# Who adds the weight sums of the seven-part products: VectorE at fixed places in place of GpSimd, in a one-layer hybrid encoder kernel

## The chip, the cores and the metric

The kernel runs on one core of a Trainium2 chip. The metric is the device time of one execution in microseconds (us); lower is better. The profile names the core's engines: PE is TensorE (matmuls), PEld its weight loads, DVE is VectorE, ACT is ScalarE, POOL is GpSimd, SP is SyncE, whose queue only issues transfers.

## The reference, cut to what matters

One layer over 256 tokens of width 4096, in float32. A combined projection feeds forgetting attention, an RWKV-7 scan and a gate; their gated outputs go through one output projection and a LayerNorm.

```python
proj = jnp.einsum('bsd,dc->bsc', x, w_in)
...
h = jnp.concatenate([fox_out, rwkv_out], axis=-1) * jax.nn.silu(z.astype(f32))
out = jnp.einsum('bsc,cd->bsd', h.astype(x.dtype), w_out)
x = _layernorm(ALPHA * x.astype(f32) + out.astype(f32), ln_gain, ln_bias, LN_EPS).astype(x.dtype)
```

`w_in` has 4096 rows and about 14,500 columns, `w_out` is 4096 by 4096. Reading and multiplying by these two is most of the work.

## The kernel before

**Two stages.** The input projection runs first, over eight groups of heads (`n` from 0 to 7), each in four blocks of 512 columns (`b` from 0 to 3; the text calls them first to fourth block). A block accumulates over 32 row tiles, taken in 16 pairs (`q`). Then comes the output projection.

**A weight pair** is one 512 KB load on SP's queue. Float32 accuracy is had from a high and a low part: ScalarE casts the pair to the high part (`split`, L155), VectorE subtracts it to get the low part (L156), and TensorE does three matmuls for each row tile and token half (`mm`, L161 to L163), twelve a pair. `weights()` keeps three split pairs ready ahead of TensorE; there are four buffers for high and three for low parts.

**Side work in slots.** After every sixth matmul of a pair, thus twice a pair and 32 times a block, `slot()` lets each side generator in `sides` take one step: first `ahead()` (preparing heads), then `gates()` (the forget gate, in group 0), `chain()` (the RWKV work, `rwkv(n)`), `weight_sums()`, and after these the generators that unload blocks and do attention. What a step issues stands in the program behind the splits made so far, and each engine works through its own instructions in that order. So a generator's place in time is set by how many slots it waits (`wait(n)`).

In the third block of a group, `chain()` multiplies the keys' tiles (`gp`, L586), masks the result on VectorE (`gb` and `lt`, L603 and L611), writes it to memory as `nd` and reads it back spread over the partitions as `Nb` (L606, L607; 1 MB a group). The triangular solve (L653, L656) runs on VectorE in the fourth block and the start of the next group; its result goes through memory again (`td` from `xc`, then `T`, L663 and L665), and `T` feeds the matmuls `qt` (L691). GpSimd scales `BK` (L588), mixes `vs` with its shifted copy (L590 to L592) and makes copies between partitions: `hr` (L512), `BKt` (L623), `pT` (L815).

At a block's end ScalarE copies the two accumulators out (`bk`, L1114). There are three such banks, so the second half of the next block's first pair waits for the first of these copies.

**Seven-part products.** In the output projection, two pairs of column blocks (those that start at 3 and 5) do the products of row-tile pairs 4 to 11 as 2 by 2 block products with seven instead of eight multiplications. These need sums of weights. There are 16 sets of them (two starts, eight row-tile pairs), and `weight_sums()` makes them while the input projection runs: for each set it loads four 128x512 tiles of `w_o` into the one buffer `ts` (four transfers of 256 KB, issued from ScalarE's queue by `send`, L846), subtracts four times in place (L856), and writes the four results to memory as two stores of 512 KB (`td`, again from ScalarE's queue). The output projection reads them back in place of plain weights.

Before, GpSimd does the subtractions, and the generator goes on at its own pace: two slots for each load and six more, six after each subtraction and six more, five after each store. That is 54 slots a set, so the sets drift through the groups: one begins 1 2/3 blocks after the other.

Of the kernel before, what the change touches and what calls it, by code (L numbers as in the profile page):

```python
# [14 lines left out]
ALU = mybir.AluOpType  # L15
# [6 lines left out]
G = 16  # L22
# [29 lines left out]
TAIL = 3  # L52
STARTS = (3, 5)
RING = (4, 3)
W = {"fo": 7, "vs": 2, "np": 4, "gp": 5, "tp": 4, "d1": 8, "d2": 12, "xp": 3, "fs": 4, "fp": 5}
NB = D // OB

# [37 lines left out]
def layer(ctx: ExitStack, tc: tile.TileContext, xt, xtok, w_main, w_lora, w_first, muv, w_o, up, par, mulora, fbias, lng, lnb, cst, out):  # L95
    nc = tc.nc
# [8 lines left out]
    def pst(name):  # L105
        return ps.tile([P, 512], F32, tag="ps", name=name)
# [52 lines left out]
    def mm(acc, at, k, hi, lo, o, n):  # L159
        tt = slice(at * P, (at + 1) * P)  # L160
        nc.tensor.matmul(acc[:, :n], xs[k][:, 0, tt], hi[:, o : o + n], start=(k == 0), stop=False)  # L161
        nc.tensor.matmul(acc[:, :n], xs[k][:, 1, tt], hi[:, o : o + n], start=False, stop=False)  # L162
        nc.tensor.matmul(acc[:, :n], xs[k][:, 0, tt], lo[:, o : o + n], start=False, stop=(k == KT - 1))  # L163

    def steps(n, last):
        both = [(j, m) for j in range(n) for m in range(2)]
        return sorted(both, key=lambda t: t[1]) if last else both
# [35 lines left out]
    nc.vector.memset(gneps, GN_EPS)  # L203

    sides = []

    def wait(n):
        for _ in range(n):
            yield
# [4 lines left out]
    def slot():  # L214
        with tc.issue_after(latest[0].ins), tc.issue_after(latest[1].ins):
            for g in list(sides):
                try:
                    next(g)
                except StopIteration:
                    sides.remove(g)  # L220
# [14 lines left out]
    tds = {(b, q): dram.tile([P, 4, OB], F32, name=f"td{b}_{q}") for b in STARTS for q in FEW}  # L235
# [22 lines left out]
    def load():  # L258
        name, src = stream.pop()
        wide = rpool is not None  # L260
        turn_of[0] = (turn_of[0] + 1) % (sum(RING) if wide else RING[0])
        own = turn_of[0] >= RING[0]
        raw = (rpool if own else wpool).tile([P, 1024], F32, tag="we" if own else "wr", name=name, bufs=RING[own])
        nc.sync.dma_start(out=raw[:, : src.shape[1] * OB], in_=src.rearrange("p k c -> p (k c)"))
        raws[name] = raw

    def fetch():
        while len(raws) < (3 if rpool is None else sum(RING) - 1) and stream:
            load()
        job = jobs.pop()  # L270
        name = job[0] if len(job) == 1 else named(*job)
        raw = raws.pop(name)
        if name not in kept:
            ready.append((job, *split(raw, OB if job[0] == "e2" else 2 * OB, name)))
            return
        hl = []
        for j in range(4):
            hl.append(xpool.tile([P, OB], F32R, tag=f"x{4 * kept[name] + j}", name=f"{name}_{j}"))
        for j in range(2):
            r = raw[:, j * OB : (j + 1) * OB]  # L280
            nc.scalar.copy(hl[j], r)
            nc.vector.tensor_tensor(hl[2 + j], r, hl[j].bitcast(F32), ALU.subtract)
        ready.append((job, hl[:2], hl[2:]))

    def weights(job):
        while len(ready) < 3 and jobs:
            fetch()
        got, hi, lo = ready.pop(0)
        assert got == job
        return hi, lo  # L290

    def block(n, b):
        if n == 0 and b == 0:
            return acc_0
        acc = [pp.tile([P, 512], F32, tag="pp", name=f"acc{n}_{b}_{m}") for m in range(2)]
        for q in range(KT // 2):
            hi, lo = weights((f"w{n}_{b}_{q}",))
            for t, (j, m) in enumerate(steps(2, q in (0, KT // 2 - 1))):
                mm(acc[m], m, 2 * q + j, hi, lo, j * OB, OB)
                if t % 2:  # L300
                    slot()
                    if n == G // 2 - 1 and b == 3:
                        paced(2 * q + t // 2)
        return acc
# [141 lines left out]
    def ch(t):  # L446
        return t.rearrange("p (c t) -> p c t", t=C)
# [70 lines left out]
    def left(t, j):  # L518
        return t.rearrange("p u c (x j t) -> p u c j x t", x=2, j=2)[:, :, :, j]

    def prepare(i):
# [30 lines left out]
        for j in range(2):  # L552
            h = HALF[j]
            nc.vector.tensor_tensor(BK[h, :, KB[j][1]], ch(k)[h], ch(eI)[h], ALU.mult)
        yield from wait(W["np"] if n else 2 * W["np"])
        nc.vector.tensor_tensor(hr[:, 0, :], hr[:, 0, :], hr[:, 1, :], ALU.add)
# [15 lines left out]
    def rwkv(n):  # L572
# [5 lines left out]
        lt = [left(LT, j) for j in range(2)]  # L578
        yield from wait(W["gp"])
        gp = [[pst(f"gp{n}_{u}_{j}") for j in range(2)] for u in range(2)]  # L580
# [34 lines left out]
        UV = [UVt[:, :, :, j, :] for j in range(2)]  # L615
        yield from wait(W["tp"])
        BKt = rp.tile([P, 2, NCH - 1, P], F32, tag="shl", name=f"BKt{n}")
# [3 lines left out]
        for a in range(4):  # L621
            for b in range(4):
                nc.gpsimd.tensor_copy(BKt[B * b : B * (b + 1), :, :, B * a : B * (a + 1)], BK[B * a : B * (a + 1), :, : NCH - 1, B * b : B * (b + 1)])  # L623
            if a % 2:
                yield
        yield from wait(W["d1"])

# [43 lines left out]
        for j in range(2):  # L671
# [8 lines left out]
            nc.gpsimd.memset(SV[j][HALF[j], :, 0, :], 0.0)  # L680
        yield from wait(W["d2"] - 1)
        for a in range(4):
# [25 lines left out]

        yield from wait(W["xp"])
        xp = pst(f"xp{n}")  # L710
# [129 lines left out]
        yield from forget()  # L840

    def weight_sums():
        g = nc.gpsimd.tensor_tensor

        def send(out, src):
            tc.keep_in_program_order(nc.scalar.dma_start(out=out, in_=src))  # L846

        for b, q in tds:
            t = rp.tile([P, 4, OB], F32, tag="ts", name=f"ts{b}_{q}")
            for n in range(4):  # L850
                send(t[:, n], w_o[b + n // 2][:, 2 * q + n % 2, :])
                yield from wait(2)
            yield from wait(6)
            b11, b21, b12, b22 = (t[:, n] for n in range(4))
            for o, x, y in ((b11, b12, b11), (b12, b22, b12), (b22, b22, b11), (b21, b21, b22)):
                g(o, x, y, ALU.subtract)  # L856
                yield from wait(6)
            yield from wait(6)
            for n in (2, 0):
                send(tds[b, q][:, n : n + 2], t[:, n : n + 2])  # L860
                yield from wait(5)
# [77 lines left out]
    def paced(k):  # L939
        while len(sent_h) < min(FAR, k * PACE[0] // PACE[1]):  # L940
            sent_h.append(len(sent_h))
            get_h(sent_h[-1])
# [155 lines left out]
    side(gates())  # L1098
    side(chain())
    side(weight_sums())  # L1100
    vt = None
    for n in range(G // 2):
        for b in range(4):
            acc = block(n, b)
            while unloading or b == 2 and n not in turned:
                slot()
            bk = rp.tile([P, 2, OB], F32, tag="bk", name=f"bk{n}_{b}") if n or b else bk_0
            for m in range(2):
                if b == 1:
                    nc.scalar.copy(bk[:, m, : 2 * P], acc[m][:, : 2 * P])  # L1110
                elif not n and not b:
                    nc.scalar.copy(bk[:, m, P:], acc[m][:, :LB])
                else:
                    nc.scalar.copy(bk[:, m, :], acc[m])  # L1114
            if b == 0:
                muvs[n] = rp.tile([P, 2 * P], F32, tag="prod", name=f"muv{n}")
                nc.sync.dma_start(out=muvs[n], in_=muv[n : n + 1, :].to_broadcast([P, 2 * P]))
            if b == 1:
                vd = vds[n % 2]
                bks[n] = bk[:, :, : 2 * P]  # L1120
                nc.sync.dma_start(out=vd[1:].rearrange("(m p) c -> p m c", m=2), in_=bk[:, :, : 2 * P])
                vs_[n] = rp.tile([P, 2, 2 * P], F32, tag="vs", name=f"vs{n}")
                nc.sync.dma_start(out=vs_[n], in_=vd[:S].rearrange("(m p) c -> p m c", m=2))
                while n and 2 * n - 1 not in foxed:
                    slot()
                vt = rp.tile([P, 2, 2 * P], F32, tag="vt", name=f"vt{n}")
                for m in range(2):
                    nc.scalar.copy(vt[:, m, :], acc[m][:, 2 * P :])
            if b != 1:
                unloading.append(n)  # L1130
                side(unload(n, b, bk, vt))
# [55 lines left out]
    for kind, b, q in plan:  # L1187
# [3 lines left out]
        if pair:  # L1191
            n = count[pair] = count[pair] + 1
# [149 lines left out]
    o = slice((NB - 1) * OB, NB * OB)  # L1342
# [96 lines left out]
```

## Time and profile before

| | |
|---|---|
| median of 3 runs | 1931.33 us (1927.58 to 1933.35) |
| the profiled execution | 1930.38 us |
| its span, first to last instruction | 1928.6 us |
| mean granted clock of TensorE | 0.997 |
| subtractions of the sets on POOL (L856) | 64, of 1279 ns at least and 1353 in the median |
| loads of the sets | 64, from 67.0 to 1294.2 us |
| stores of the sets | 32, from 128.9 to 1353.7 us |

A line of the page that groups instructions reads: line, engine, operation, output from inputs by the program's names, shapes, count, then busy time and mean duration in ns, then the idle time of the engine ahead of them and what ended most of it. A line of the waits reads: engine and line, what it waited for, total us, how many times, the longest. A line of the timeline: start and duration in us, engine, line, operation, and in brackets the idle time before it and what ended it; ACTq and SPq are the parts of ScalarE and SP that issue transfers. A line of the windows: the stretch, its length, busy time of PE, PEld, DVE, ACT and POOL with the number of instructions, granted clock, the DMA engines' busy share, and GB/s. DMA lines of the page end with the median time from issue to landing.

### The profile page before, as it was taken

To read this page: it belongs to the slowest core of one execution; us is meant where nothing else is said; L and a number is where in the kernel's file an instruction comes from. 1 tells how busy PE (TensorE), PEld (TensorE's weight loads), DVE (VectorE), ACT (ScalarE), POOL (GpSimd) and SP (SyncE) were. 2 spreads that over 40 slices of the span, in tenths; PEclk is the share of its full clock that TensorE was granted. 3 is DMA by queue.
4 is the path that set the end of the run, shared out by engine and by line. 5 is a ranking of instruction groups with operands and counts; after the bars stand their busy time and mean duration, and the time that the engine had idled before them with its cause. 6 is when DMAs were issued, how large, how long until landed. Compare 5 with 4: busy or idle time off the path is not lost.

```text
span 1928.6 us, 28470 instructions
## 1 busy us (share of the span) xinstructions
PE 1905.0 (99%) x9745; PEld 1574.9 (82%) x9745; DVE 1489.4 (77%) x2469; ACT 1012.8 (53%) x1581; POOL 356.9 (19%) x530
## 2 busy tenths in 40 slices
PE   9999999999999999999999999999999999999998
PEld 9887788888778888887878888888888878878885
DVE  7678778786878687867786878788768775887886
ACT  6554465456535564565355545654565454455552
POOL 0223123120331223213220331232002200000000
PEclk9999999999999999999999999999999999999999
DMA  9678777877787788867887787788767875778883
GB/s 344 190 238 252 227 203 256 249 243 217 233 249 236 220 267 250 253 193 248 246 250 219 246 268 235 221 272 241 235 188 221 288 268 179 265 256 300 293 301 120
DMA packets 288262, 466.76 MB, mean 242 GB/s; under 512 B 144434, under 2 KB 171716, under 8 KB 288116
## 3 DMA queue, kind: packets, MB, share of 16 engines
q1 hardware_dynamic: 274004, 431.03, 72.3%
q10 hardware_dynamic: 14112, 33.90, 4.9%
q8 instruction: 76, 1.25, 0.2%
q14 instruction: 70, 0.57, 0.1%
HBM read 418.43 MB, written 46.42 MB: 241 GB/s over the span
## 4 chain that ended last, share of the span: by engine, by line
PE 90%; DVE 5%; DMA 2%; ACT 1%; issue 1%; SPq 0%; DVEq 0%; POOL 0%; ACTq 0%; POOLq 0%
PE acc L161 22%; PE acc L163 22%; PE acc L162 22%; PE oacc L980 4%; PE oacc L983 4%; PE oacc L981 4%; DMA w<-in_w_main_dram 1%; PE rh L700 1%; PE p L980 1%; PE p L983 1%; PE p L981 1%; PE gp L586 1%; PE up L731 1%; PE sp L741 1%; DVE prod L653 1%
## 5 line engine op out<-in xcount | busy, mean ns | idle before, releaser
L856 POOL TENSOR_TENSOR ts<-ts 128x512 f32<-128x512 f32 x64 | 103.0, 1609 | 251.4 <-DMA ts<-in_w_o_dram 248.4
L815 POOL COPY pT<-lg 32x96 f32<-32x96 f32 x128 | 58.7, 458 | 426.1 <-DVE lg L811 421.4
L653 DVE TENSOR_TENSOR prod<-Nb,xc 128x8 f32<-128x8 f32 (+30 forms) x248 | 83.4, 336 | 3.0
L623 POOL COPY BKt<-BK 32x192 f32<-32x192 f32 x128 | 70.4, 550 | 53.5 <-DVE BK L620 48.5
L656 DVE TENSOR_REDUCE xc<-prod 128x8 f32<-128x16 f32 (+30 forms) x248 | 72.6, 293 | 6.5
L156 DVE TENSOR_TENSOR w_0l<-w,w_0h 128x1024 fp32r<-128x1024 f32 x31 | 39.2, 1266 | 40.8 <-ACT w_0h L155 34.1
L155 ACT CAST w_0h<-w 128x1024 fp32r<-128x1024 f32 x31 | 32.5, 1048 | 64.5 <-DMA w<-in_w_main_dram 57.7
L155 ACT CAST w_6h<-w 128x1024 fp32r<-128x1024 f32 x31 | 32.7, 1055 | 47.1 <-PE acc L162 26.9
L155 ACT CAST w_8h<-w 128x1024 fp32r<-128x1024 f32 x31 | 32.6, 1052 | 45.7 <-DMA w<-in_w_main_dram 16.8
L156 DVE TENSOR_TENSOR w_9l<-w,w_9h 128x1024 fp32r<-128x1024 f32 x31 | 39.1, 1260 | 19.6 <-ACT w_9h L155 8.7
L156 DVE TENSOR_TENSOR w_6l<-w,w_6h 128x1024 fp32r<-128x1024 f32 x31 | 43.0, 1387 | 13.3 <-ACT hry L774 7.3
L1290 POOL CAST zah<-mv 128x1 fp32r<-128x1 f32 x1 | 0.2, 188 | 284.5 <-DVE mv L1285 284.5
L156 DVE TENSOR_TENSOR w_15l<-w,w_15h 128x1024 fp32r<-128x1024 f32 x31 | 39.6, 1277 | 16.5 <-issue 12.6
L156 DVE TENSOR_TENSOR w_11l<-w,w_11h 128x1024 fp32r<-128x1024 f32 x31 | 38.4, 1239 | 17.7 <-PE acc L163 12.0
L156 DVE TENSOR_TENSOR w_10l<-w,w_10h 128x1024 fp32r<-128x1024 f32 x31 | 38.4, 1238 | 17.1 <-ACT w_10h L155 8.1
L155 ACT CAST w_10h<-w 128x1024 fp32r<-128x1024 f32 x31 | 32.6, 1052 | 35.1 <-DMA w<-in_w_main_dram 27.1
L161 PE MATMUL acc<-w_0h,x 128*128 128x512 f32 x124 | 49.9, 403 | 1.1 <-ACT bk L1114 1.0
L163 PE MATMUL acc<-w_5l,x 128*128 128x512 f32 x124 | 48.7, 392 | 1.6 <-DVE w_5l L156 1.6
L155 ACT CAST w_1h<-w 128x1024 fp32r<-128x1024 f32 x31 | 32.7, 1054 | 33.4 <-DMA w<-in_w_main_dram 15.7
L161 PE MATMUL acc<-w_15h,x 128*128 128x512 f32 x124 | 50.1, 404 | 0.0
L155 ACT CAST w_9h<-w 128x1024 fp32r<-128x1024 f32 x31 | 32.6, 1050 | 33.3 <-DMA w<-in_w_main_dram 17.6
L161 PE MATMUL acc<-w_9h,x 128*128 128x512 f32 x124 | 50.0, 403 | 0.0
(1052 smaller groups left out, 6834.6 us busy)
## 6 DMA issues: line engine op xcount, KB each, us to landing
w<-in_w_main_dram SPq DMA_DIRECT2D x496, 512.0 KB, 4.5
wo<-in_w_o_dram SPq DMA_DIRECT2D x96, 512.0 KB, 4.9
ts<-in_w_o_dram ACTq DMA_DIRECT2D x64, 256.0 KB, 3.7
td<-ts ACTq DMA_DIRECT2D x32, 512.0 KB, 4.4
e<-td SPq DMA_DIRECT2D x32, 512.0 KB, 5.2
bt<-bk SPq DMA_DIRECT2D x88, 128.0 KB, 4.5
Nb<-nd SPq DMA_DIRECT2D x16, 512.0 KB
e<-in_w_o_dram SPq DMA_DIRECT2D x16, 512.0 KB, 4.0
```

Of the source, the lines that this page charges most:

```text
L155: latest[1] = nc.scalar.copy(hi[:, :n], src[:, :n])
L156: latest[0] = nc.vector.tensor_tensor(lo[:, :n], src[:, :n], hi[:, :n].bitcast(F32), ALU.subtract)
L161: nc.tensor.matmul(acc[:, :n], xs[k][:, 0, tt], hi[:, o : o + n], start=(k == 0), stop=False)
L162: nc.tensor.matmul(acc[:, :n], xs[k][:, 1, tt], hi[:, o : o + n], start=False, stop=False)
L163: nc.tensor.matmul(acc[:, :n], xs[k][:, 0, tt], lo[:, o : o + n], start=False, stop=(k == KT - 1))
L623: nc.gpsimd.tensor_copy(BKt[B * b : B * (b + 1), :, :, B * a : B * (a + 1)], BK[B * a : B * (a + 1), :, : NCH - 1, B * b : B * (b + 1)])
L653: first = nc.vector.tensor_tensor(prod[:, :, :, s + 1 :], nb[:, :, s : s + 1, s + 1 :].to_broadcast([P, 2, NJ, w]), xc[:, :, :, s + 1 :], ...
L656: solved = nc.vector.tensor_reduce(xc[:, :, :, s : s + 1], prod[:, :, :, s:], AX.X, ALU.add)
L856: g(o, x, y, ALU.subtract)
L980: nc.tensor.matmul(acc, h, hi, start=n[0] == n[1], stop=False)
L981: nc.tensor.matmul(acc, l, hi, start=False, stop=False)
L983: nc.tensor.matmul(acc, h, lo, start=False, stop=not n[0])
```

## The change

The four subtractions of each set move from GpSimd to VectorE. They no longer come a fixed number of slots after the loads. The generator now holds after its loads until the input projection has reached pair 7 (`CALM`) of a given block: in groups 1 to 7 the first and the third block, in group 0 (whose first block has no slots) the second and the third. `where[0]` is the block and pair that `block()` is working on. From there the subtractions follow two slots apart (slots 14, 16, 18 and 20 of the block), the two stores go out at slots 26 and 31, and the next set's loads at slots 36, 38, 40 and 42, which are slots 4 to 10 of the next block. The loads' and stores' engine, sizes and number stay.

```diff
+CALM = 7
...
     sides = []
+    where = [(0, 0, 0)]
...
             hi, lo = weights((f"w{n}_{b}_{q}",))
+            where[0] = n, b, q
...
     def weight_sums():
-        g = nc.gpsimd.tensor_tensor
-
         def send(out, src):
             tc.keep_in_program_order(nc.scalar.dma_start(out=out, in_=src))
 
-        for b, q in tds:
+        places = [(n, b, CALM) for n in range(G // 2) for b in (0 if n else 1, 2)]
+        for (b, q), place in zip(tds, places, strict=True):
             t = rp.tile([P, 4, OB], F32, tag="ts", name=f"ts{b}_{q}")
             for n in range(4):
                 send(t[:, n], w_o[b + n // 2][:, 2 * q + n % 2, :])
                 yield from wait(2)
-            yield from wait(6)
+            while place > where[0]:
+                yield
             b11, b21, b12, b22 = (t[:, n] for n in range(4))
             for o, x, y in ((b11, b12, b11), (b12, b22, b12), (b22, b22, b11), (b21, b21, b22)):
-                g(o, x, y, ALU.subtract)
-                yield from wait(6)
-            yield from wait(6)
+                nc.vector.tensor_tensor(o, x, y, ALU.subtract)
+                yield from wait(2)
+            yield from wait(4)
             for n in (2, 0):
                 send(tds[b, q][:, n : n + 2], t[:, n : n + 2])
                 yield from wait(5)
```

## The prediction

> **What bounds the kernel now.** I began with the page: busy times, the chain, and the group of the line that the change touches.
>
> ```profile
> PE 1905.0 (99%) x9745; PEld 1574.9 (82%) x9745; DVE 1489.4 (77%) x2469; ACT 1012.8 (53%) x1581; POOL 356.9 (19%) x530
> PE 90%; DVE 5%; DMA 2%; ACT 1%; issue 1%; SPq 0%; DVEq 0%; POOL 0%; ACTq 0%; POOLq 0%
> L856 POOL TENSOR_TENSOR ts<-ts 128x512 f32<-128x512 f32 x64 | 103.0, 1609 | 251.4 <-DMA ts<-in_w_o_dram 248.4
> ```
>
> TensorE is busy almost throughout, and the chain runs through it for nine tenths. POOL has 81% of the span free, so taking 103 us from it is worth nothing by itself. The change can only pay where the sums, or their transfers, hold TensorE up. So I read what TensorE waited for.
>
> ```profile
> PE lp L482 <- DVE upl L474: 2.9, 2, 2.3
> PE qt L691 <- DMA T<-td: 2.0, 2, 1.0
> PE acc L163 <- DVE w_7l L156: 1.6, 1, 1.6
> PE acc L161 <- ACT bk L1114: 1.0, 1, 1.0
> PE acc L163 <- DVE w_12l L156: 0.8, 1, 0.8
> ```
>
> These are few and short, but they aren't the whole loss. Groups 1 to 7 do identical work, so I cut the span at the start of each block and compared like with like (columns: stretch, length, busy time per engine, granted clock, DMA share, GB/s).
>
> ```profile
> 207.82:261.98 54.16, 52.15 (x297) 43.02 (x296) 35.88 (x61) 24.50 (x40) 6.78 (x6) 0.97 0.75 226
> 404.09:455.13 51.04, 50.77 (x297) 41.52 (x296) 37.92 (x66) 25.26 (x43) 4.00 (x5) 1.00 0.69 199
> 984.17:1035.34 51.17, 50.83 (x297) 41.44 (x296) 37.96 (x69) 25.70 (x45) 1.40 (x3) 1.00 0.73 214
> 1175.07:1225.25 50.18, 50.18 (x298) 41.68 (x296) 34.56 (x62) 25.40 (x43) 5.44 (x5) 1.00 0.79 244
> 310.29:359.03 48.74, 47.09 (x231) 38.53 (x230) 40.68 (x49) 21.37 (x30) 22.39 (x29) 1.00 0.76 239
> 503.27:553.76 50.49, 48.20 (x231) 39.76 (x230) 37.55 (x52) 18.70 (x25) 17.36 (x27) 0.97 0.65 208
> 888.86:938.54 49.68, 47.05 (x231) 38.39 (x230) 39.64 (x50) 22.23 (x35) 22.82 (x29) 1.00 0.72 224
> 1463.23:1509.69 46.46, 46.46 (x231) 38.53 (x230) 35.90 (x46) 21.39 (x31) 17.49 (x24) 1.00 0.70 209
> 553.76:600.59 46.83, 45.47 (x201) 37.09 (x200) 43.14 (x89) 26.24 (x44) 11.55 (x12) 1.00 0.88 267
> 938.54:984.17 45.63, 45.18 (x202) 37.18 (x200) 37.42 (x81) 21.85 (x36) 10.26 (x12) 1.00 0.89 269
> 1320.02:1364.91 44.89, 44.89 (x202) 37.26 (x201) 37.77 (x87) 23.48 (x37) 4.34 (x10) 1.00 0.85 246
> ```
>
> The first four are first blocks (groups 1, 2, 5, 6), the next four third blocks (1, 2, 4, 7), the last three fourth blocks (2, 4, 6). Each kind has an undisturbed length: 50.18, 46.46 and 44.89 us. The excess over it is what can be won. First blocks: 3.98 + 0.86 + 0.99 = 5.8. Third: 2.28 + 4.03 + 3.22 = 9.5. Fourth: 1.94 + 0.74 = 2.7. Together 18.0 us; the other blocks of these kinds, and the second blocks, are within some tenths of undisturbed.
>
> **Are the sums behind this excess?** The disturbed third blocks are the ones in which POOL's sums run while VectorE is full. Group 4's, around 902 us, beside a split of group 7 with POOL quiet:
>
> ```profile
> 902.55 2.21 DVE L156 TENSOR_TENSOR w_5l<-w,w_5h 128x1024 fp32r<-128x1024 f32 x1
> 902.19 1.48 POOL L856 TENSOR_TENSOR ts<-ts 128x512 f32<-128x512 f32 x1
> 909.44 0.89 POOL L512 COPY hr<-hr 32x16 f32<-32x16 f32 x4
> 910.36 0.17 DVE L556 TENSOR_TENSOR hr<-hr 128x16 f32<-128x16 f32 x1 [3.38 <-POOL hr L512]
> 1483.82 1.22 DVE L156 TENSOR_TENSOR w_9l<-w,w_9h 128x1024 fp32r<-128x1024 f32 x1
> ```
>
> Beside POOL's adds a split takes 2.21 instead of 1.22 us. Further, the short copies of hr wait in POOL's queue behind the sums and the products of vs (L590 to L592), and VectorE waits 3.38 us for them, with w_7l's split queued behind that: that is TensorE's 1.6 us wait. The products of vs stay on POOL; but the undisturbed third blocks hold them too, without this loss, so it takes both. Group 2's 4.03 us has TensorE's 2.3 us wait for upl at its start; after that pause the granted clock of its block is 0.97. I book the 9.5 us as removable.
>
> In group 1's first block it is the sums' stores:
>
> ```profile
> 213.30 0.33 ACTq L846 DMA_DIRECT2D td<-ts  x1
> 215.94 4.67 DMA td<-xc
> td<-xc SPq DMA_DIRECT2D x16, 64.0 KB, 1.5
> ```
>
> The solve's small write lands after 4.67 instead of 1.5 us, right behind a 512 KB store of the sums, and TensorE waits for T. In the new order nothing of the sums lies in a first block's pairs 0 to 6, so I book these 4.0 us as removed too. Groups 2 and 5 lose 0.9 and 1.0 us in first blocks in which VectorE is 3.4 us busier than in the undisturbed one (37.9 against 34.56): again adds on POOL beside a full VectorE, and again gone. What the fourth blocks lose (2.7 us) is the stores' doing, below; I count it as removed here and as a cost there.
>
> **The change, part by part.**
>
> *Off POOL:* 64 adds of 1609 ns. Nothing is gained but what VectorE loses beside them, booked above.
>
> *Onto VectorE:* 64 adds of two SBUF tensors. The nearest row is this one, with the same shape:
>
> ```profile
> L1084 DVE TENSOR_TENSOR res<-res,lg 128x512 f32<-128x512 f32 x15 | 9.9, 685 | 0.0
> ```
>
> 64 x 0.685 = 44 us. What hides it is the idle time of VectorE at the places. The four adds of a set go into weight pairs 7, 8, 9 and 10, one each. Those pairs in an undisturbed first block, a third block, the three pairs behind these, and group 0's third block:
>
> ```profile
> 1384.79:1395.20 10.41, 10.41 (x81) 8.61 (x80) 6.47 (x10) 4.88 (x10) 0.00 (x0) 1.00 0.83 212
> 1483.00:1493.37 10.37, 10.37 (x69) 8.54 (x68) 6.67 (x9) 3.20 (x4) 1.40 (x1) 1.00 0.76 235
> 1493.37:1501.53 8.16, 8.16 (x37) 6.76 (x36) 7.52 (x10) 3.14 (x3) 1.56 (x3) 1.00 0.61 142
> 144.73:154.04 9.31, 8.46 (x37) 6.68 (x36) 9.18 (x15) 3.15 (x3) 0.00 (x0) 1.00 0.73 182
> ```
>
> In a first block VectorE has 10.41 - 6.47 = 3.9 us free in pairs 7 to 9: all adds fit, cost 0. In a third block pairs 7 to 9 have 3.7 us free, the next three 0.64. The third add can land behind the masks of gp (the same slot, the solve's side step first) and the fourth in pair 10, so up to 1.4 us are pushed into pairs 10 to 12. They are covered by the weights split ahead: three pairs are kept ready, so a split may come some 2 to 3 us late before TensorE runs out. Cost 0 in groups 1 to 7; were that cover gone, 0.7 to 1.4 us a block.
>
> Group 0 has no such room: from pair 10 of its third block VectorE is busy 9.18 of 9.31 us (the forget gate's steps share it), and TensorE already waits 0.8 us for w_12l. The two late adds cost between 0 and 1.4; I take +1.0. Group 0's other set sits in its second block, where POOL's adds of the first set now run in the same pairs: what VectorE gets back there is of the size of what it takes on. I take 0; at worst none of it is hidden, 4 x 0.685 = 2.7.
>
> What stands behind an add that waits are VectorE's splits, and behind them TensorE. But no add should wait:
>
> ```profile
> ts<-in_w_o_dram ACTq DMA_DIRECT2D x64, 256.0 KB, 3.7
> ```
>
> A load lands in 3.7 us, and each set's loads go out a block or more before its adds. Only group 0 is closer: its first loads go out in pairs 0 to 3, its second set's in pairs 2 to 5, of the block of their adds. A pair without side matmuls takes 8.16 / 3 = 2.7 us (third row of the fence above), so the last load, two pairs ahead, has 5.4 us.
>
> *The loads and stores, moved along.* ScalarE's queue still issues them, but at other times: stores at slots 26 and 31 of the block with the adds (pairs 13 and 15), the next loads in pairs 2 to 5 of the block after. In first blocks this is quiet. In third blocks the first store falls, every time, into the stretch in which Nb is fetched and the next block's w_0 stands behind it. Before shows this once, in group 2 (ScalarE and the SP queue; then the same stretch of group 7, without a store):
>
> ```profile
> 540.59 1.53 SPq L607 DMA_DIRECT2D Nb<-nd  x2
> 542.91 0.35 ACTq L846 DMA_DIRECT2D td<-ts  x1
> 552.34 1.05 ACT L155 CAST w_0h<-w 128x1024 fp32r<-128x1024 f32 x1 [8.43 <-DMA w<-in_w_main_dram]
> 553.62 0.33 ACTq L846 DMA_DIRECT2D td<-ts  x1
> 550.00:554.00 4.00, 4.00 (x20) 3.29 (x18) 0.58 (x1) 1.51 (x2) 1.73 (x5) 1.00 0.91 370
> 1495.90 1.61 SPq L607 DMA_DIRECT2D Nb<-nd  x2
> 1505.30 1.05 ACT L155 CAST w_0h<-w 128x1024 fp32r<-128x1024 f32 x1 [5.46 <-DMA w<-in_w_main_dram]
> ```
>
> w_0 is there 9.40 us after Nb's issue in group 7, 11.75 in group 2: the store made it 2.35 us later. Counted from the next block's start (553.76 and 1509.69), w_0 came 1.42 us ahead instead of 4.39, so 2.97 us later (Nb itself was late), and the block lost 1.94 us, because ScalarE's bk copies stand behind w_0 and TensorE's second half waits for their bank. So about 1.0 us of lateness is free. With 2.35 us from the store alone, a block loses 1.3. If the store costs only its own transfer time, 0.524 MB at 370 GB/s = 1.4 us, it loses 0.4. I take the middle, 0.85, since both describe the same event: 7 groups x 0.85 = +6.0. Ends: 0 (the 1.0 us covers all; not below, since an undisturbed fourth block has no wait to give back) and 7 x 1.94 = +13.6. Group 0's fourth block already has ts loads in that stretch: 0.
>
> The Trainium skill ("DMA: Bandwidth & Descriptors", section on queues, rings and completion order) says that a DMA engine takes turns between the queues it has work for, a packet at a time. By that rule the store costs its transfer time and no more, and the sum would be -18.0 + 1.0 + 7 x 0.4 = -14.2 us, on the edge of rival A. By group 2's row alone, 1.3 us a block, it would be -7.9; the trace so far speaks for more than the rule.
>
> **The sum.** -18.0 + 1.0 + 6.0 = -11.0 us. The profiled execution took 1930.38 us (span 1928.6, 1.8 around it), 0.95 below the median of the runs, 1931.33. That gives 1919.4 on its scale and **1920** on the median's. With all the lower ends the sum is -18.0, with all the upper ones -18.0 + 13.6 + 1.4 + 2.7 = -0.3.
>
> **The rivals.**
>
> *A, the stores are nearly free* (0 to 0.4 us a block). For: w_0's spare 1.0 us, and the transfer time. Against: group 2's 2.35 us. -18.0 + 1.0 + 7 x 0.2 = -15.6, so 1916.
>
> *B, the win is handed back:* each third block's store costs what group 2's did, 1.94 us. For: it is the very slot that recurs. Against: Nb was itself late there, by VectorE's backlog, which goes. -18.0 + 1.0 + 13.6 = -3.4, so 1928: no change that can be told.
>
> *C, slower:* both stores of a third block hurt, the first w_0 and the second, right behind w_1's cast, the loads of w_3 and w_4. At twice 1.94, 3.9 us, in 8 fourth blocks: -18.0 + 1.0 + 31 = +14, so 1945. It decides above 18.0 + 5.8 = 24 us, 3 us a block. Against: in group 2 the second store went out just so, at 553.62 us, and the whole block lost 1.94.
>
> That the change wouldn't do what it says I give no chance: each add's place is in the program order of its engine.
>
> **How the numbers follow.** A measurement of this kernel tells 0.3% from no change, 5.8 us. Forecast (0.4 to 1.3 us a block) 0.54, A 0.19, B 0.18, C 0.09. Faster: forecast and A, 0.73; same: B, 0.18; slower: C, 0.09. The range goes from A's lower end, 1931 - 18 = 1913, a microsecond below for the small excess of second blocks (1912), to the upper ends' sum, 1931; C is left out.
>
> **What the new profile would show.** POOL's busy time down by about 103 us, VectorE's up, by less than 44 since its splits shrink; L156 groups all near 1.22 us a split; first blocks of groups 1 to 7 at 50.2 us and third blocks at 46.5. If third blocks are longer, the late adds weren't covered. Fourth blocks at 45.7 bear out the middle price, 44.9 rival A, 46.8 rival B, 48 and more C. The forecast fails if first blocks keep their excess (then the stores weren't its cause), or if DMA waits turn up in second blocks, where I booked none.

## The result, and the profile after

The changed kernel takes 1920.29 us (median of 5 runs, 1916.57 to 1921.64) against 1931.33 before (5 runs, 1927.58 to 1933.35): ratio 0.9942, 95% interval 0.9926 to 0.9959. The forecast was 1920. The profiled execution took 1921.64 us, 8.7 less than the one of before.

The page of the changed kernel (L847 and L859 are now the lines of the sets' transfers and adds, L157 that of a split's low part):

```profile
span 1919.9 us, 28355 instructions
PE 1901.6 (99%) x9745; PEld 1572.3 (82%) x9745; DVE 1490.2 (78%) x2533; ACT 1013.0 (53%) x1581; POOL 284.1 (15%) x466
...
PE 87%; DVE 5%; DMA 5%; ACT 1%; issue 1%; SPq 1%; DVEq 0%; ACTq 0%; POOL 0%
...
td<-ts ACTq DMA_DIRECT2D x32, 512.0 KB, 8.3
```

The chain has lost TensorE's share to transfers (DMA 5% where it was 2%). A store of the sets lands in 8.3 us in the median where it was 4.4; the trace tells the landing of six of the 32 only (before, of four), here the first stores of third blocks. POOL's busy time fell by 73 us only, not by the 103 that its adds had taken: its masking of nb takes 10.7 us more than before, and its copies of hr, BKt and pT 4 to 5 us more each. VectorE took on 64 adds and is busy 0.8 us longer than before. The groups of its instructions say why:

```profile
L859 DVE TENSOR_TENSOR ts<-ts 128x512 f32<-128x512 f32 x64 | 43.7, 682 | 0.0
...
L157 DVE TENSOR_TENSOR w_6l<-w,w_6h 128x1024 fp32r<-128x1024 f32 x31 | 38.8, 1250 | 12.6 <-PE acc L164 12.6
...
L157 DVE TENSOR_TENSOR w_5l<-w,w_5h 128x1024 fp32r<-128x1024 f32 x31 | 38.0, 1225 | 5.3 <-PE acc L164 3.4 <-issue 1.4
```

The adds cost 43.7 us, 682 ns each (predicted 685). VectorE's other work fell by as much, 42.9 us, and without any adds (an experiment below) VectorE is busy 1452.9 us, 36.5 less than before: that is about what GpSimd's adds had done to it. The w_6l splits, for one, fell from 1387 ns on average to 1250, w_5l from 1351 to 1225, the undisturbed length being 1.22 us.

The blocks, in the order in which the prediction showed them (first blocks of groups 1 and 2; third blocks of 1, 2 and 4; fourth blocks of 2, 3 and 4; last the third block of group 0):

```profile
208.74:259.79 51.05, 49.93 (x293) 41.36 (x292) 36.54 (x66) 22.94 (x38) 1.79 (x2) 1.00 0.72 212
399.78:450.03 50.25, 50.25 (x298) 41.61 (x296) 36.95 (x68) 24.46 (x42) 1.40 (x2) 1.00 0.78 223
308.43:354.90 46.47, 46.47 (x232) 38.55 (x230) 38.83 (x51) 21.10 (x31) 17.11 (x23) 1.00 0.73 228
498.20:544.67 46.47, 46.47 (x231) 38.55 (x230) 36.92 (x49) 19.33 (x25) 15.90 (x25) 1.00 0.71 219
882.43:928.90 46.47, 46.47 (x232) 38.54 (x231) 37.99 (x50) 20.68 (x28) 17.48 (x23) 1.00 0.74 228
544.67:592.19 47.52, 45.82 (x201) 36.97 (x200) 38.57 (x89) 25.60 (x44) 5.01 (x8) 1.00 0.88 259
737.08:784.01 46.93, 45.70 (x202) 37.02 (x200) 38.16 (x87) 25.37 (x43) 5.01 (x8) 1.00 0.87 258
928.90:975.18 46.28, 45.63 (x202) 37.02 (x201) 37.37 (x86) 24.43 (x42) 6.53 (x11) 1.00 0.86 256
115.20:163.19 47.99, 46.55 (x227) 37.87 (x226) 40.99 (x60) 21.17 (x28) 15.23 (x19) 1.00 0.79 244
```

Every third block of groups 1 to 7 now has the undisturbed length, the first blocks all but that of group 1 to within 0.1 us. The fourth blocks of groups 2 to 6 are longer than before, by 0.6 to 2.0 us; those of groups 1 and 7 aren't. What TensorE waited for:

```profile
PE acc L164 <- DVE w_11l L157: 2.3, 4, 0.7
PE acc L162 <- ACT bk L1117: 2.0, 3, 1.0
PE acc L164 <- DVE w_12l L157: 1.4, 1, 1.4
PE qt L694 <- DMA T<-td: 1.1, 1, 1.1
```

The waits for upl and w_7l are gone; w_12l is group 0's, up from 0.8; the first two lie in fourth blocks.

I cut every profile below at the starts of its blocks in the same way. These are sums over groups 1 to 6 (the ends of the seventh group differ), in us. Group 0 is counted from the start of its second block, and so is the last column, up to the start of the input projection's last matmul with a high part:

| kernel | first | second | third | fourth | group 0 | whole stage |
|---|---|---|---|---|---|---|
| before | 306.9 | 289.6 | 288.3 | 272.2 | 138.9 | 1486.1 |
| changed | 302.3 | 289.5 | 278.8 | 277.1 | 139.7 | 1477.7 |
| changed, second profile | 302.0 | 289.5 | 278.9 | 275.2 | 140.9 | 1476.8 |
| no sets at all | 301.7 | 289.0 | 278.8 | 269.3 | 138.7 | 1467.8 |

(The second profile and the kernel without sets are experiments below. The last column also holds group 7.)

### The profile page after: what moved, and what is told of

Its sections match the earlier page's. It is cut to its first block, busy times and chain, and to the rows that moved or that the text cites. A ratio compares the mean times of both kernels' runs of the same rounds, so it can differ in the third digit from the quotient of the medians.

```text
span 1919.9 us, 28355 instructions
## 1 busy us (share of the span) xinstructions
PE 1901.6 (99%) x9745; PEld 1572.3 (82%) x9745; DVE 1490.2 (78%) x2533; ACT 1013.0 (53%) x1581; POOL 284.1 (15%) x466
## 4 chain that ended last, share of the span: by engine, by line
PE 87%; DVE 5%; DMA 5%; ACT 1%; issue 1%; SPq 1%; DVEq 0%; ACTq 0%; POOL 0%
PE acc L162 22%; PE acc L164 21%; PE acc L163 21%; PE oacc L983 5%; PE oacc L986 4%; PE oacc L984 4%; DMA w<-in_w_main_dram 3%; PE rh L703 1%; PE p L983 1%; PE p L986 1%; PE p L984 1%; PE gp L589 1%; PE up L734 1%; PE sp L744 1%; DVE prod L656 0%
## 5 line engine op out<-in xcount | busy, mean ns | idle before, releaser
L818 POOL COPY pT<-lg 32x96 f32<-32x96 f32 x128 | 62.8, 491 | 640.8 <-DVE lg L814 636.0
L626 POOL COPY BKt<-BK 32x192 f32<-32x192 f32 x128 | 74.9, 585 | 67.5 <-DVE BK L623 62.6
L656 DVE TENSOR_TENSOR prod<-Nb,xc 128x8 f32<-128x8 f32 (+30 forms) x248 | 73.1, 295 | 3.0
L157 DVE TENSOR_TENSOR w_0l<-w,w_0h 128x1024 fp32r<-128x1024 f32 x31 | 38.2, 1231 | 33.5 <-ACT w_0h L156 30.1
L157 DVE TENSOR_TENSOR w_9l<-w,w_9h 128x1024 fp32r<-128x1024 f32 x31 | 38.0, 1225 | 25.6 <-ACT w_9h L156 9.2
L157 DVE TENSOR_TENSOR w_8l<-w,w_8h 128x1024 fp32r<-128x1024 f32 x31 | 37.7, 1215 | 20.0 <-ACT w_8h L156 17.8
L162 PE MATMUL acc<-w_15h,x 128*128 128x512 f32 x124 | 50.2, 405 | 0.0
L162 PE MATMUL acc<-w_14h,x 128*128 128x512 f32 x124 | 50.0, 403 | 0.0
L164 PE MATMUL acc<-w_11l,x 128*128 128x512 f32 x124 | 47.5, 395 | 2.5 <-DVE w_11l L157 2.3
L164 PE MATMUL acc<-w_12l,x 128*128 128x512 f32 x124 | 48.5, 391 | 1.4 <-DVE w_12l L157 1.4
L157 DVE TENSOR_TENSOR w_11l<-w,w_11h 128x1024 fp32r<-128x1024 f32 x31 | 37.9, 1223 | 15.0 <-issue 6.6
L515 POOL COPY hr<-hr 32x16 f32<-32x16 f32 x64 | 45.2, 706 | 28.1 <-DVE hr L512 25.7
L157 DVE TENSOR_TENSOR w_10l<-w,w_10h 128x1024 fp32r<-128x1024 f32 x31 | 37.9, 1222 | 14.5 <-issue 5.9
```

The costliest lines, as they stand in the source:

```text
L157: latest[0] = nc.vector.tensor_tensor(lo[:, :n], src[:, :n], hi[:, :n].bitcast(F32), ALU.subtract)
L656: first = nc.vector.tensor_tensor(prod[:, :, :, s + 1 :], nb[:, :, s : s + 1, s + 1 :].to_broadcast([P, 2, NJ, w]), xc[:, :, :, s + 1 :], ...
L818: (nc.gpsimd.tensor_copy if b % 2 else nc.scalar.copy)(pT[B * b : B * (b + 1), :, B * a : B * (a + 1)], lg[B * a : B * (a + 1), :, B * b : ...
```

## The experiments

**My theory** was the prediction's: GpSimd's adds held up a full VectorE, which explains the long third blocks, and the fourth blocks now pay for the stores. **The rivals:** the place does it and not the engine; the adds still cost on VectorE; the fourth block's excess isn't the sets' doing. The first four kernels ran on one chip, beside runs of before with a median of 1929.22 us.

### The engine undone, the places kept

```diff
-                nc.vector.tensor_tensor(o, x, y, ALU.subtract)
+                nc.gpsimd.tensor_tensor(o, x, y, ALU.subtract)
```

> The changed kernel with the adds back on GpSimd, at the changed kernel's places (pairs 7 to 10 of the same blocks); loads and stores as there. It tells the engine from the place. My theory is that adds on POOL cost only where VectorE is full: first blocks then stay near 50.2 us, third blocks, where the third and fourth add meet the masks, lose up to 1 us each, and the time is 1921 to 1926. Rival 'the place does it all': same as the changed kernel, 1920 within 2 us, no block longer. Rival 'the engine does it all': back near 1931.

1925.87 us, ratio 0.9983 (0.9973 to 0.9992). Inside my numbers, but not for my reason. POOL's timeline, in group 2:

```profile
468.53 1.28 POOL L859 TENSOR_TENSOR ts<-ts 128x512 f32<-128x512 f32 x1 [3.62 <-DMA ts<-in_w_o_dram]
473.50 4.17 POOL L859 TENSOR_TENSOR ts<-ts 128x512 f32<-128x512 f32 x3 [3.69 <-DMA ts<-in_w_o_dram]
561.31 6.26 POOL L859 TENSOR_TENSOR ts<-ts 128x512 f32<-128x512 f32 x4 [12.81 <-DMA ts<-in_w_o_dram]
```

These adds belong into the third block and the next group's first; they ran in the second and the fourth, as soon as their loads had landed. A place in the program order holds an instruction only behind what its own engine still has to do, and POOL had nothing. So this run doesn't keep the place. It shows the old harm at new spots: second blocks went up to 292.9 us in sum, and group 0's third block to 49.84, with one wait of 3.3 us for w_12l.

### The place undone, the engine kept

```diff
 (the kernel before)
-        g = nc.gpsimd.tensor_tensor
+        g = nc.vector.tensor_tensor
```

> The kernel before with nothing changed but the engine: VectorE adds, at the old drifting pace of 54 slots a set. My theory: an add on VectorE costs 0.685 us of it and nothing to its neighbours, so the blocks that were long through POOL's adds shrink (third blocks of groups 1, 2 and 4 by 1 to 3 us each), while stores that fall badly stay where they were (group 1's first block 54 us): 1921 to 1927. Rival 'the place does it all': 1930 or more, because the adds land where VectorE is full.

1920.82 us, ratio 0.9957 (0.9944 to 0.9970), not to be told from the change itself. Third blocks of groups 1, 2 and 4, and the fourth of group 2:

```profile
306.95:353.79 46.84, 46.84 (x231) 38.51 (x230) 39.53 (x53) 22.84 (x35) 17.21 (x22) 1.00 0.81 259
497.59:544.06 46.47, 46.47 (x232) 38.53 (x230) 36.35 (x50) 19.53 (x25) 16.18 (x25) 1.00 0.73 225
880.32:926.78 46.46, 46.46 (x231) 38.53 (x230) 38.13 (x55) 22.32 (x35) 17.14 (x22) 1.00 0.76 240
544.06:591.85 47.79, 45.71 (x202) 36.97 (x201) 39.24 (x88) 25.57 (x43) 6.48 (x8) 1.00 0.87 255
```

One word of the program brings the third blocks down (279.2 us in sum), though the adds fall anywhere. The rival that the place does it all is out. Group 2's fourth block keeps its excess: the store stands where it stood. In the other groups it drifts past, and the fourth blocks sum to 272.6 instead of the change's 277.1.

One expectation failed, and it bears on the prediction: group 1's first block was to stay at 54 us, since the stores in it stay. They did, 0.2 and 5.5 us into the block as before, but the block is short, and TensorE waits 0.2 us for T in it instead of 2.0:

```profile
212.85 0.33 ACTq L846 DMA_DIRECT2D td<-ts  x1
207.37:258.63 51.26, 50.95 (x297) 41.93 (x296) 35.79 (x64) 24.64 (x40) 1.69 (x2) 1.00 0.80 237
```

### No adds

```diff
-            for o, x, y in (...):
-                nc.vector.tensor_tensor(o, x, y, ALU.subtract)
-                yield from wait(2)
-            yield from wait(4)
+            yield from wait(12)
```

> The changed kernel with the 64 adds left out: the sets are loaded and stored at the same slots, and the output projection reads plain weights where sums belong. It measures what the adds still cost. My theory (idle time and the weights split ahead cover them, group 0's third block excepted): 1918 to 1920, group 0's third block about 1 us shorter, all else as in the changed kernel. Rival 'the late adds eat the cover that the fourth blocks then lack': fourth blocks drop to 45 us and the time is 1914 or less.

1918.06 us, ratio 0.9943 (0.9927 to 0.9958): as the change, so the adds are hidden to within what this can tell. Group 0's third block took 47.36 instead of 47.99 us. Fourth blocks came down to 273.9 in sum, not to the floor; the spread between two profiles of the change (277.1 and 275.2) is too wide to give that to the adds.

### No sets

```diff
-        return tds[b, q][:, 2:4] if kind == "e3" else tds[b, q][:, 0:2]
+        return w_o[b][:, two, :] if kind == "e3" else w_o[b + 1][:, two, :]
...
-    side(weight_sums())
```

> The changed kernel without the sets' work: no loads, adds or stores of them, and the output projection reads plain weights of the same size in their place. It is the floor. My theory, that the fourth blocks' excess in the changed kernel (up to 2.6 us each) comes from the stores and loads of the sets: all fourth blocks of groups 1 to 6 at 44.9 us, time 1908 to 1912. Rival 'that excess is not theirs' (the fourth block is simply full): fourth blocks still at 46 us on average, time 1917 to 1920.

1912.23 us, ratio 0.9911 (0.9899 to 0.9923). Group 1's first block, and group 2's fourth:

```profile
207.58:258.44 50.86, 50.51 (x298) 41.73 (x296) 34.60 (x61) 24.53 (x40) 1.07 (x2) 1.00 0.68 198
542.89:587.78 44.89, 44.89 (x202) 37.25 (x201) 37.87 (x88) 24.51 (x42) 4.88 (x8) 1.00 0.80 236
```

All fourth blocks of groups 1 to 6 take 44.9 us, so the excess is the sets' doing, and 6 to 8 us are left between the change and this floor (by the two ratios, and by the medians of two chips). The 0.7 us of group 1's first block are not theirs.

**Which of the sets' transfers is it?** The adds being hidden, the next four kernels moved stores, loads and places (one chip, before 1930.16 us).

### Stores early

```diff
                 nc.vector.tensor_tensor(o, x, y, ALU.subtract)
-                yield from wait(2)
-            yield from wait(4)
+                yield
+            yield from wait(2)
             for n in (2, 0):
                 send(tds[b, q][:, n : n + 2], t[:, n : n + 2])
-                yield from wait(5)
+                yield from wait(2)
+            yield from wait(12)
```

> The changed kernel with the four adds one slot apart (slots 14 to 17) and the stores at slots 20 and 22 instead of 26 and 31, ahead of the fetch of Nb; the next loads still at slots 36 to 42. My theory: in the changed kernel the fourth blocks lose 7.8 us (groups 1 to 6), part of it because the stores make w_0 and with it the bk copies late (2.0 us of TensorE's waits for bk), part because of the loads (2.3 us of waits for w_11l). Then the waits for bk go, fourth blocks lose 3 to 6 us, and the time is 1916 to 1919; the adds close together push VectorE by at most 0.5 us ahead of the masks, which costs nothing. Rival 'only the amount of transfers counts': 1920, fourth blocks as before; its other form, nd's small packets held up by the second store, would make Nb late and fourth blocks longer, 1922 or more.

1912.05 us, ratio 0.9903 (0.9890 to 0.9917): better than I expected, and as good as the kernel without sets. It beats both kernels. Group 2's third and fourth block, and what TensorE still waited for longest:

```profile
495.70:542.16 46.46, 46.46 (x231) 38.53 (x230) 38.33 (x50) 20.57 (x27) 16.49 (x25) 1.00 0.75 232
542.16:587.05 44.89, 44.89 (x201) 37.24 (x200) 37.77 (x88) 24.55 (x43) 5.31 (x9) 1.00 0.87 260
```

```profile
PE acc L164 <- DVE w_12l L157: 1.1, 1, 1.1
```

All fourth blocks are at 44.9 us, waits for bk and w_11l are both gone, and the loads are still in pairs 2 to 5. How the store acts is seen in group 2, SP's and ScalarE's rows of the changed kernel, then of this one:

```profile
531.64 1.53 SPq L610 DMA_DIRECT2D Nb<-nd  x2
533.82 0.33 ACTq L847 DMA_DIRECT2D td<-ts  x1
542.59 1.05 ACT L156 CAST w_0h<-w 128x1024 fp32r<-128x1024 f32 x1 [7.78 <-DMA w<-in_w_main_dram]
546.59 0.58 ACT L1117 COPY bk<-acc 128x512 f32<-128x512 f32 x1
```

```profile
521.02 0.33 ACTq L847 DMA_DIRECT2D td<-ts  x1
528.79 0.33 ACTq L847 DMA_DIRECT2D td<-ts  x1
529.51 3.37 SPq L610 DMA_DIRECT2D Nb<-nd  x2
538.18 1.05 ACT L156 CAST w_0h<-w 128x1024 fp32r<-128x1024 f32 x1 [5.87 <-DMA w<-in_w_main_dram]
542.66 0.58 ACT L1118 COPY bk<-acc 128x512 f32<-128x512 f32 x1
```

From Nb's issue, w_0 comes after 10.95 us with a store behind Nb and after 8.67 without; bk follows at 14.95 and 13.15, which is 1.92 and 0.50 us into the next block. In group 5 w_0 isn't late, and w_1 is. The same rows of the changed kernel, then of this one:

```profile
1106.10 1.53 SPq L610 DMA_DIRECT2D Nb<-nd  x2
1109.22 0.33 ACTq L847 DMA_DIRECT2D td<-ts  x1
1114.73 1.05 ACT L156 CAST w_0h<-w 128x1024 fp32r<-128x1024 f32 x1 [4.52 <-DMA w<-in_w_main_dram]
1118.63 1.05 ACT L156 CAST w_1h<-w 128x1024 fp32r<-128x1024 f32 x1 [2.85 <-DMA w<-in_w_main_dram]
```

```profile
1098.13 2.47 SPq L610 DMA_DIRECT2D Nb<-nd  x2
1107.36 1.05 ACT L156 CAST w_0h<-w 128x1024 fp32r<-128x1024 f32 x1 [5.45 <-DMA w<-in_w_main_dram]
1108.59 1.06 ACT L156 CAST w_1h<-w 128x1024 fp32r<-128x1024 f32 x1 [0.18 <-DMA w<-in_w_main_dram]
```

w_0 comes after 8.63 us against 9.23, w_1 after 12.53 against 10.46, and the bk copies stand behind w_1 too.

### Loads late

```diff
+            yield from wait(20 if place[0] else 0)
```

(behind the stores, which stay at slots 26 and 31)

> The changed kernel with the next set's loads 20 slots later, in pairs 12 to 15 of the block behind the stores instead of pairs 2 to 5 (groups 1 to 7); stores unchanged. My theory: TensorE's waits for w_11l in fourth blocks go (they follow a late w_8, queued behind bt's writes and the loads); waits for bk stay; fourth blocks of groups 1 to 6 lose 2 to 4 us instead of 7.8, the time is 1915 to 1918. Rival 'only the amount counts': 1920, and the waits turn up at the start of the next first blocks, which then exceed 50.2 us.

1921.57 us, ratio 0.9953 (0.9941 to 0.9966): the time that I expected, 1915 to 1918, is missed. In the fourth blocks it went as the theory had it: waits for bk stay (2.6 us), those for w_11l are gone in groups 1 to 7, and the sum is 273.2, 3.9 over the floor. But the moved loads cost 2 us elsewhere, in waits for w_5l in third blocks. Whether the loads share in the excess this run can't tell: two kernels below whose loads and stores both stay at their slots have fourth blocks of 273.1 and 272.7 us.

```profile
PE acc L162 <- ACT bk L1118: 2.6, 3, 1.0
PE acc L164 <- DVE w_5l L157: 1.9, 3, 0.9
```

### Both

> Both edits: adds one slot apart, stores at slots 20 and 22, loads in pairs 12 to 15 of the next block. My theory, that the fourth blocks' excess is one part stores and one part loads: it goes down to 0 to 2 us over groups 1 to 6, and the time is 1912 to 1915, close to the kernel without the sets' work (1912). Rival 'only the amount counts': 1918 or more.

1914.84 us, ratio 0.9917 (0.9903 to 0.9931). Inside the expected numbers, but the late loads win nothing over early stores alone, which were 2.8 us faster: fourth blocks sum to 269.7 where early stores alone gave 269.3, and third blocks to 280.7 where they gave 278.8.

### The second block in place of the third

```diff
-        places = [(n, b, CALM) for n in range(G // 2) for b in (0 if n else 1, 2)]
+        places = [(n, b, CALM) for n in range(G // 2) for b in ((0, 1) if n else (1, 2))]
```

> The changed kernel with the second place of groups 1 to 7 in the second block instead of the third (pair 7 there): stores at the end of first and second blocks, loads at the start of second and third ones, nothing of the sets in fourth blocks after group 0. My theory: fourth blocks at 44.9 us, first and third blocks unchanged, second blocks up by 0 to 0.5 us each since VectorE is full in pair 7 and from pair 10 on but free in pairs 8 and 9; 1912 to 1916. Rival 'every block pays for the transfers that it is given': third blocks 47 us or more, 1919 to 1922.

1924.50 us, ratio 0.9965 (0.9951 to 0.9978), far from my 1912 to 1916. Fourth blocks are at 44.9 as I expected, but second blocks are 0.8 to 1.5 us longer each than without sets, beyond my 0.5, and third blocks sum to 282.0 instead of 278.8:

```profile
451.55:500.71 49.16, 48.50 (x275) 40.04 (x274) 39.13 (x66) 31.20 (x54) 9.28 (x21) 1.00 0.80 231
```

and among TensorE's waits

```profile
PE acc L164 <- DVE w_13l L157: 4.2, 7, 0.9
PE acc L164 <- DVE w_5l L157: 2.7, 4, 1.5
```

Seven waits for w_13l, one in each second block of groups 1 to 7: two free pairs weren't room enough for four adds. This is what an unhidden add looks like. The four waits for w_5l lie in third blocks, which now hold loads; the rival, which had third blocks at 47 us or more, is borne out in four of the seven.

**The last four** took the early stores apart, and came back to the engine (one chip, before 1929.92 us).

### Adds close, stores unmoved

```diff
-                yield from wait(2)
-            yield from wait(4)
+                yield
+            yield from wait(8)
```

> The changed kernel with the four adds one slot apart (slots 14 to 17), everything else at its old slot: stores at 26 and 31. It is the half of the early-stores kernel that isn't the stores. My theory, that the stores' time made that kernel's gain: as the changed kernel, 1918 to 1922, fourth blocks of groups 1 to 6 still 4 to 9 us over 44.9 in sum. Rival 'the adds' spacing made it' (the late adds held up the splits behind the masks): 1911 to 1914, fourth blocks at 44.9.

1919.74 us, ratio 0.9942 (0.9926 to 0.9957), fourth blocks 273.1 in sum, 3.8 over the floor and not at it. The spacing of the adds isn't what the early stores gained by.

### The first store early

```diff
             for n in (2, 0):
                 send(tds[b, q][:, n : n + 2], t[:, n : n + 2])
-                yield from wait(2)
-            yield from wait(12)
+                yield from wait(11 if n else 5)
```

(against the kernel with early stores)

> As the early-stores kernel, but only the first store of a set goes out at slot 20; the second stays at slot 31, behind w_1's cast. My theory, as in the prediction: it is the first store that makes w_0 late; TensorE's waits for bk go, and the second store alone costs 0 to 0.3 us a fourth block: 1912 to 1914. Rival 'the second store holds up the weights behind it', which would account for the waits for w_11l: fourth blocks 3 to 5 us over in sum, 1915 to 1917.

1914.96 us, ratio 0.9920 (0.9904 to 0.9935), a microsecond over my numbers. Group 2's fourth block:

```profile
544.41:589.29 44.88, 44.88 (x201) 37.20 (x200) 37.12 (x86) 23.56 (x38) 4.81 (x8) 1.00 0.87 257
```

All fourth blocks of groups 1 to 6 are at 44.9 us. It is the first store, in the stretch of Nb, that costs; the second, behind w_1, costs those blocks nothing. The waits for w_11l are gone from them too, with the loads where they were: in the change it took the first store to make them. The last 3 us to 1912 lie outside these blocks (1.2 us in one third block, 1.0 in group 1's first, 1.7 in group 0's fourth, which also lies behind a second store, so there it isn't shown to be free), and the two kernels' intervals overlap.

### The change again

> The changed kernel once more, unaltered, to have it on the same chip and against the same runs of before as its two variants: 1918 to 1922.

1920.03 us, ratio 0.9945 (0.9931 to 0.9960).

### POOL's adds, held at the places

```diff
-                nc.vector.tensor_tensor(o, x, y, ALU.subtract)
+                nc.vector.tensor_copy(x[0:1, 0:1], x[0:1, 0:1])
+                nc.gpsimd.tensor_tensor(o, x, y, ALU.subtract)
```

> The changed kernel with the adds on GpSimd, each held at its place by a one-element copy on VectorE of an input of the add (the earlier run with POOL at the places showed that POOL ran its adds as soon as the loads landed, wherever the program had put them). It tells the place from the engine. My theory, that POOL's adds cost only where VectorE is full: first blocks 50.2 to 50.6, second blocks back at 48.2, third blocks 46.5 to 47.5, together 1919 to 1924. Rival 'adds on POOL cost wherever they are': 1926 or more.

1918.43 us, ratio 0.9941 (0.9926 to 0.9956): as the change on the same chip. The adds (shortest, median and longest, in ns), then the third blocks of groups 2 and 4:

```profile
L860 POOL TENSOR_TENSOR ts<-ts x64: 1264/1291/2167, 99.1 to 1484.8; 128x512 f32<-128x512 f32 x64
```

```profile
498.10:544.62 46.52, 46.52 (x231) 38.53 (x230) 36.03 (x49) 19.39 (x25) 22.99 (x29) 1.00 0.72 219
880.35:926.82 46.47, 46.47 (x232) 38.53 (x230) 35.39 (x50) 20.01 (x26) 23.58 (x29) 1.00 0.73 224
```

With the place truly kept, POOL does no harm there: first blocks from group 2 on 50.2 us, third 46.5, and second blocks, which the run without the hold had brought to 292.9 us in sum, 289.5. Its adds take 1291 ns in the median and 1429 on average; before, 1353 and 1609.

## Why the prediction was right, point by point

**Third blocks, -9.5 us.** Measured: from 288.3 to 278.8, -9.5. That the adds on POOL at their old places were the cause is now shown from both sides: the engine alone takes it away (1920.82), and the held place alone does (1918.43). So half of the change would have done, and the two cures don't add up. Two things in the prediction's account stay short. Group 2's long third block holds none of the sums but the last 1.2 us of one: the four run from 496.1 to 504.4 us, at the end of the block ahead, and the wait for upl comes behind them. Group 5's first block lies just so behind four adds (977.8 to 984.9 us). And no run parts the two ways in which POOL held VectorE up, longer splits and copies of hr queued behind the adds.

**First blocks, -5.8 us.** Measured -4.6. The term was too large by group 1's block, 51.05 us: without any sets it still takes 50.86, so 0.7 us of its excess was never the sets'. Nor were the stores shown to make the rest: with VectorE adding at the old pace they stand at the same places in this block, and it takes 51.26 us instead of 54.16. 2.0 us of the 54.16 are TensorE's longer busy time at a granted clock of 0.97. What made this block long stays open. That those of groups 2 and 5 would come to 50.2 held.

**The adds on VectorE, 0.** 682 ns each, covered, as the kernel without them shows. The cover is thin: in second blocks it is gone at once.

**Group 0, +1.0.** Measured 139.7 - 138.9 = +0.8: +0.7 in the third block, where it was booked (without the adds that goes), +0.4 in the fourth, booked at nothing, and -0.2 in the second. In the second profile it is +2.0, with +1.6 in the fourth.

**Fourth blocks, -2.7 + 6.0 = +3.3.** Measured from 272.2 to 277.1, +4.9, and +3.0 in the second profile. In group 2 the mechanism was as predicted, down to the bk copies, and its row, 11.75 us from Nb to w_0 before, came back as 10.95. But I had priced the second way in which it shows, the waits for w_11l, at nothing, and looked for their cause in the loads; they go when the first store does, with the loads in place, and whether the loads share in them isn't told. Group 7's fourth block, which I had counted in, is as long as before. Per block it is 1.3 and 1.0 us in the two profiles, where I took 0.85.

What a store costs can be read over both profiles of the change, groups 1 to 7. The first store always goes out 10.85 us ahead of the next block; Nb goes out about 14 us ahead of it in nine of the fourteen cases, so 3.0 to 3.1 us ahead of the store, and about 13 in five, 2.0 to 2.4 us ahead. In the five w_0 comes 10.0 to 11.4 us after Nb's issue, in the nine after 8.5 to 9.6, which is as without stores (7.9 to 9.5 in the kernels with no sets and with early stores). But w_1 comes after 11.0 to 12.9 us in all fourteen, against 9.2 to 10.8 without. So the lateness is there every time, 1.7 to 1.9 us of w_1 on average, and Nb's own time says whether w_0 has it already. The five blocks behind lose 2.1 us on average, the nine 0.4. A late Nb alone costs nothing: in the kernel without sets it goes out 13.2 and 13.1 us ahead in groups 2 and 3, whose fourth blocks take 44.9. I had read a price of the store off w_0 of one group alone.

The Trainium skill ("DMA: Bandwidth & Descriptors", queues, rings and completion order) has the DMA engines take turns between queues packet by packet; I had weighed its price, the transfer time of 1.4 us, against group 2's 2.35. The 1.7 to 1.9 us of w_1 are nearer to the rule's price.

**The sum.** -8.7 us in the profiled execution and -11.0 between the medians, against -11.0. In the profile the first blocks gave 1.2 us less than booked and the fourth cost 1.6 more. That the medians agree to a tenth is luck: two profiled runs of the change differ by 1.4 us.

**Rivals.** A (nearly free stores) and C (stores that cost 3 us a block) are out for this kernel; with the stores at slots 20 and 22 they are free as A had it, and 1912.05 us is under the 1916 I gave it. B's 1.94 us a block was reached in some blocks (2.63 and 2.04 in groups 2 and 3) and not on average.

## What to carry to other kernels

Where work is moved to an engine's idle stretch, ask first what it was harming: an engine with 80% of its time free can still be the one that holds up the full engine beside it. A step that recurs at a fixed place repeats its collisions in every round, where a drifting one meets them now and then, so check the place of each transfer, and not just of the arithmetic; here moving two stores by six and nine slots was worth 7 to 8 us, against the 10 to 11 of the whole change, and the first of them gave more than half of it. And a place in the program order is kept by an engine only if it has work or a wait in front of it.

## What the runs showed of the hardware

A GpSimd add and a VectorE subtraction that meet lengthen each other: in before, splits of 1.22 us take up to 2.32 and adds of 1.28 up to 2.83; held at the places, adds take up to 2.17. The Trainium skill ("SBUF — State Buffer", section "Who interferes with whom") says that a VectorE instruction with two SBUF inputs and a GpSimd instruction that reads SBUF exclude each other for a whole instruction. The trace agrees in size: the longest splits of before are a split and nearly one add of 1.28. I hadn't expected the near balance: 44 us of adds were added to VectorE and its busy time rose by 0.8.

The granted clock of two blocks of before, which hold pauses of TensorE (two of 1.0 us, and one of 2.3), read 0.97; in the change every block of the input projection reads 1.00. The length of a pause alone doesn't decide it. With the adds close, group 1's first block reads 0.97 with a pause of 1.3 us; with POOL at the places, group 0's third block reads 1.00 with one of 3.3. In the two blocks of before TensorE was busy 2.0 and 1.7 us longer than in undisturbed ones, so 3.7 of the 18.0 us that the prediction booked as removable were matmul time and not waits.
